# Nearest-neighbour upsampling by two on one core: eight loads of falling size in place of four equal ones

## The chip, the core and the metric

The kernel runs on one core of a Trainium2 chip. The metric is the device time of one execution in microseconds (us). Four executions of the kernel before took 199.92 to 200.24 us, with a median of 200.06. A profile comes from one execution, and its span is the part of that execution between the first and the last recorded work.

## The reference

```python
batch, channels, h, w = (16, 64, 64, 64)        # x, float32
new_h, new_w = (h * scale_factor, w * scale_factor)   # scale_factor = 2
for i in range(new_h):
    for j in range(new_w):
        result[:, :, i, j] = x[:, :, i // scale_factor, j // scale_factor]
```

Every input element is written four times, into a square of two by two. The input has 65,536 rows of 64 numbers (16.78 MB), the output 67.11 MB. Nothing is calculated; the work is moving and repeating.

## The kernel before, in words

The input is seen as 65,536 rows. They are cut into four blocks (`NB`) of 128 partitions x 128 rows, so that a partition's part of a block is 128 neighbouring rows, 32 KiB in one piece. The output is seen the same way: one input row becomes two output rows, 1 KiB in one piece.

**Loads.** Lines 65 to 68 issue all four loads on SP's queue before anything else. Each block has a tile `xt` of its own, so no load waits for anything. The first of these loads is moved by `begin_before_barrier` (lines 9 to 27) to a place ahead of the barrier with which the program begins; it takes the first SP instruction of the body, whatever that is, as long as it is a load without waits.

**Copies.** Lines 74 to 86 go through the four blocks, and in each through four pieces of `K` = 32 rows per partition. For a piece, a tile `u` of 32 KiB per partition is filled: VectorE (DVE) expands the first `KV` = 18 rows (line 78), ScalarE (ACT) the other 14 (line 81). Both read a row with a stride that repeats it and each number in it twice. There are two `u` buffers (`bufs=2`, line 62).

**Stores.** Line 84 stores a `u` tile, again on SP's queue: 128 pieces of 32 KiB, one per partition. Since a partition owns 128 neighbouring rows of a block, the pieces of one store lie 128 KiB apart in the output. A `u` buffer may be filled again when its store has landed.

**Order.** All 20 transfers (four loads, 16 stores) are issued by SP and form one queue, which 16 DMA engines work on in parallel. Each DMA engine has its share of every transfer: eight partitions, so eight data packets and one small one that reports the end. The stores stand in the queue behind all loads.

Of the kernel before, what the change touches and what calls it, by code (L numbers as in the profile page):

```python
# [1 line left out]

# [4 lines left out]


def begin_before_barrier(nc):

    blocks = nc.main_func.blocks
    main, body = blocks[0], blocks[1]
    sp = mybir.EngineType.SP
    load = next(i for i in body.instructions if i.engine == sp)
    assert isinstance(load, mybir.InstDMACopy), type(load)
    assert not (load.sync_info and load.sync_info.on_wait)
    body.instructions = [i for i in body.instructions if i is not load]
    kept = list(main.instructions)  # L20
    at = next(
        n
        for n, i in enumerate(kept)
        if i.engine == sp and isinstance(i, mybir.InstDrain)
    )
    kept.insert(at, load)
    main.instructions = kept


@with_exitstack  # L30
def kernel(
    ctx: ExitStack,
    tc: tile.TileContext,
    x: bass.AP,
    scale_factor: int,
    out: bass.AP,
):
    nc = tc.nc
    nc.at_finalize(begin_before_barrier)
    P = nc.NUM_PARTITIONS  # L40
    s = int(scale_factor)
    B, C, H, W = x.shape
    R = B * C * H
    fdt = x.dtype

    K, J = 32, 4
    NB = R // (P * J * K)  # L50
    assert NB * P * J * K == R
    xf = x.rearrange("b c h w -> (b c h) w").rearrange(
        "(n p r) w -> n p r w", n=NB, p=P
    )
    of = out.rearrange("b c (h hd) w -> (b c h) (hd w)", hd=s).rearrange(
        "(n p r) w -> n p r w", n=NB, p=P
    )

    KV = 18

    xpool = ctx.enter_context(tc.tile_pool(name="xin", bufs=NB))
    upool = ctx.enter_context(tc.tile_pool(name="uexp", bufs=2))

    xts = []
    for n in range(NB):
        xt = xpool.tile([P, J * K, W], fdt, name="xt")
        nc.sync.dma_start(out=xt[:, :, :], in_=xf[n])
        xts.append(xt)

    def expanded(rows):  # L70
        k = rows.shape[1]
        return rows.unsqueeze(2).unsqueeze(4).to_broadcast([P, k, s, W, s])

    for n in range(NB):
        for j in range(J):
            r0 = j * K
            u = upool.tile([P, K, s, W, s], fdt, name="u")
            nc.vector.tensor_copy(  # L78
                out=u[:, :KV], in_=expanded(xts[n][:, r0 : r0 + KV, :])
            )  # L80
            nc.scalar.copy(  # L81
                out=u[:, KV:], in_=expanded(xts[n][:, r0 + KV : r0 + K, :])
            )
            nc.sync.dma_start(
                out=of[n, :, r0 : r0 + K, :], in_=u[:, :, :, :, :]
            )


# [1 line left out]
_INS = ['x', 'scale_factor']  # L90
_OUTS = [((16, 64, 128, 128), 'float32')]

_NUMBERS = {'scale_factor': 2}


# [26 lines left out]
```

## Time and profile before

| what | number |
|---|---|
| median of four executions | 200.06 us |
| the profiled execution | 200.24 us, of which the span is 198.5 us |
| DVE busy, 16 copies of 128x4608 | 40.9 us, 2560 ns each |
| ACT busy, 16 copies of 128x3584 | 50.8 us, 3179 ns each |
| loads | 4 of 4096 KB |
| stores | 16 of 4096 KB, 16.1 us from issue to landing (median) |
| DMA packets | 2880, of which 320 under 512 B and none between 512 B and 8 KB |
| HBM read, written | 16.78 MB, 67.11 MB |
| mean rate over the span | 423 GB/s |

How to read the views: an engine's busy share says how much of the span it worked. A row of 40 digits cuts the span (or a chosen stretch) into 40 equal slices, and each digit is a busy share in tenths. The GB/s row says what the DMA engines moved in each slice. The chain of work that ended last is followed back from the end: each piece has its start, its length and what it was. "SPq" and "ACTq" are the queues of instructions of SP and ACT. "Landing" is the moment at which all the data of a transfer has arrived. In slices shorter than a packet the GB/s row shows bursts and zeros, since a packet's bytes are booked whole.

### The profile page before, as it was taken

The numbers are of one execution on the slowest core, as the hardware profiler recorded it, in microseconds if no ns is written. First come the engines' busy times: TensorE is split into PE (matmuls) and PEld (weight loads), VectorE is DVE, ScalarE is ACT, GpSimd is POOL, SyncE is SP. The second block draws the span as 40 slices with busy tenths as digits, with TensorE's granted clock in tenths as the row PEclk, the third lists the DMA queues.
The fourth block names the chain that finished last, engine by engine and source line by source line (L and its number), as shares of the span: only waits on it lengthen the run. The fifth ranks groups of instructions, "written<-read, shape, count | busy, mean of one in ns | idle before, by whom it ended". The sixth has DMA issues, their size and how long they took to land.

```text
span 198.5 us, 145 instructions
## 1 busy us (share of the span) xinstructions
DVE 40.9 (21%) x16; ACT 52.0 (26%) x17; POOL 0.2 (0%) x4
## 2 busy tenths in 40 slices
DVE  0054000000405050505050505050505050404000
ACT  2057000000415150606060606060606060505000
POOL 0000000000000000000000000000000000000000
DMA  8999999999999999999999999999999999999994
GB/s 317 423 423 423 456 449 456 376 376 423 423 436 443 436 443 429 443 429 429 423 423 436 443 436 443 429 443 429 429 423 423 436 443 436 443 429 443 429 429 211
DMA packets 2880, 83.89 MB, mean 423 GB/s; under 512 B 320, under 2 KB 320, under 8 KB 320
## 3 DMA queue, kind: packets, MB, share of 16 engines
q1 hardware_dynamic: 2880, 83.89, 98.8%
HBM read 16.78 MB, written 67.11 MB: 423 GB/s over the span
## 4 chain that ended last, share of the span: by engine, by line
DMA 77%; ACT 14%; issue 0%; ACTq 0%
DMA out_dram<-u 70%; ACT u L81 14%; DMA xt<-in_x_dram 6%; ACTq L81 0%
## 5 line engine op out<-in xcount | busy, mean ns | idle before, releaser
L81 ACT COPY u<-xt 128x3584 f32<-128x3584 f32 x16 | 50.8, 3179 | 128.5 <-DMA out_dram<-u 118.3
L78 DVE COPY u<-xt 128x4608 f32<-128x4608 f32 x16 | 40.9, 2560 | 139.9 <-DMA out_dram<-u 127.6
L81 ACT ACT_TABLE_LOAD x1 | 1.3, 1283 | 0.8 <-PEq L103 0.8
L103 POOL MEMSET const-uint8-127<- 128x1 uint8 x1 | 0.1, 102 | 0.0
L103 POOL MEMSET const-bfloat16-1.0<- 128x1 bf16 x1 | 0.1, 101 | 0.0
L103 POOL MEMSET const-float32-1.0<- 128x1 f32 x1 | 0.1, 99 | 0.0
L103 POOL MEMSET const-float32-0.0<- 128x1 f32 x1 | 0.1, 98 | 0.2 <-issue 0.2
## 6 DMA issues: line engine op xcount, KB each, us to landing
out_dram<-u SPq DMA_DIRECT2D x16, 4096.0 KB, 16.1
xt<-in_x_dram SPq DMA_DIRECT2D x4, 4096.0 KB, 25.9
```

Source lines behind the costliest of these rows:

```text
L78: nc.vector.tensor_copy(out=u[:, :KV], in_=expanded(xts[n][:, r0 : r0 + KV, :]))
L81: nc.scalar.copy(out=u[:, KV:], in_=expanded(xts[n][:, r0 + KV : r0 + K, :]))
L103: nc = _bacc.Bacc("TRN2", target_bir_lowering=False, num_devices=1)
```

## The change

The rows are cut into eight blocks of 128, 128, 64, 64, 32, 32, 32 and 32 rows per partition. A block has one load, so the pieces that a load moves are 32 KiB per partition in the first two loads, 16 KiB in the next two and 8 KiB in the last four; the loads are of 4096, 4096, 2048, 2048 and four times 1024 KB. All eight are issued at the beginning, and each has a tile with a name of its own in the pool `xin` (`bufs=1`); together these take the same space as the four tiles before. The pieces of 32 rows that are expanded and stored stay 16 in number and equal in size; `KV` and the two `u` buffers stay. What a partition owns changes with the blocks: the stores of a block of 64 rows write 32 KiB pieces that lie 64 KiB apart, and the store of a block of 32 rows writes 4096 KB in one stretch. The function that moves the first load is unchanged, and the first load is the same as before.

```diff
+    blocks = [128, 128, 64, 64, 32, 32, 32, 32]
 
-    K, J = 32, 4
-    NB = R // (P * J * K)
-    assert NB * P * J * K == R
-    xf = x.rearrange("b c h w -> (b c h) w").rearrange(
-        "(n p r) w -> n p r w", n=NB, p=P
-    )
-    of = out.rearrange("b c (h hd) w -> (b c h) (hd w)", hd=s).rearrange(
-        "(n p r) w -> n p r w", n=NB, p=P
-    )
+    K = 32
+    assert P * sum(blocks) == R
 
     KV = 18
 
-    xpool = ctx.enter_context(tc.tile_pool(name="xin", bufs=NB))
+    xf = x.rearrange("b c h w -> (b c h) w")
+    of = out.rearrange("b c (h hd) w -> (b c h) (hd w)", hd=s)
+
+    def of_block(rows, first, k):
+        return rows[first : first + P * k, :].rearrange("(p k) w -> p k w", p=P)
+
+    xpool = ctx.enter_context(tc.tile_pool(name="xin", bufs=1))
     upool = ctx.enter_context(tc.tile_pool(name="uexp", bufs=2))
 
-    xts = []
-    for n in range(NB):
-        xt = xpool.tile([P, J * K, W], fdt, name="xt")
-        nc.sync.dma_start(out=xt[:, :, :], in_=xf[n])
-        xts.append(xt)
+    loaded = []
+    first = 0
+    for n, k in enumerate(blocks):
+        xt = xpool.tile([P, k, W], fdt, name=f"x{n}")
+        nc.sync.dma_start(out=xt[:, :, :], in_=of_block(xf, first, k))
+        loaded.append((xt, first, k))
+        first += P * k
 
...
-    for n in range(NB):
-        for j in range(J):
-            r0 = j * K
+    for xt, first, k in loaded:
+        for r0 in range(0, k, K):
             u = upool.tile([P, K, s, W, s], fdt, name="u")
...
             nc.sync.dma_start(
-                out=of[n, :, r0 : r0 + K, :], in_=u[:, :, :, :, :]
+                out=of_block(of, first, k)[:, r0 : r0 + K, :],
+                in_=u[:, :, :, :, :],
             )
```

More of the change, by code (lines that the diff above doesn't have):

```diff
@@ L70, in expanded @@
-    def expanded(rows):
-        k = rows.shape[1]
-        return rows.unsqueeze(2).unsqueeze(4).to_broadcast([P, k, s, W, s])
-    for n in range(NB):
-        for j in range(J):
-            r0 = j * K
+    blocks = [128, 128, 64, 64, 32, 32, 32, 32]
+    K = 32
+    assert P * sum(blocks) == R
+    KV = 18
+    xf = x.rearrange("b c h w -> (b c h) w")
+    of = out.rearrange("b c (h hd) w -> (b c h) (hd w)", hd=s)
+    def of_block(rows, first, k):
+        return rows[first : first + P * k, :].rearrange("(p k) w -> p k w", p=P)
@@ new lines @@
+    xpool = ctx.enter_context(tc.tile_pool(name="xin", bufs=1))
+    upool = ctx.enter_context(tc.tile_pool(name="uexp", bufs=2))
+    loaded = []
[5 more added lines that the diff above has]
+        first += P * k
+    def expanded(rows):
+        return rows.unsqueeze(2).unsqueeze(4).to_broadcast(
+            [P, rows.shape[1], s, W, s]
+        )
@@ L77 @@
+    for xt, first, k in loaded:
+        for r0 in range(0, k, K):
             u = upool.tile([P, K, s, W, s], fdt, name="u")
             nc.vector.tensor_copy(
-                out=u[:, :KV], in_=expanded(xts[n][:, r0 : r0 + KV, :])
+                out=u[:, :KV], in_=expanded(xt[:, r0 : r0 + KV, :])
             )
             nc.scalar.copy(
-                out=u[:, KV:], in_=expanded(xts[n][:, r0 + KV : r0 + K, :])
+                out=u[:, KV:], in_=expanded(xt[:, r0 + KV : r0 + K, :])
```

## The prediction

> **What bounds the kernel now.** I read the page's engine shares and slices first, then the chain of work that ended last, then the landings of single transfers, and at last the DMA slices around the one place where the rate dips.
>
> ```profile
> DVE 40.9 (21%) x16; ACT 52.0 (26%) x17; POOL 0.2 (0%) x4
> DMA  8999999999999999999999999999999999999994
> GB/s 317 423 423 423 456 449 456 376 376 423 423 436 443 436 443 429 443 429 429 423 423 436 443 436 443 429 443 429 429 423 423 436 443 436 443 429 443 429 429 211
> q1 hardware_dynamic: 2880, 83.89, 98.8%
> ```
>
> The copies take a quarter of the span at most; the DMA engines are at nine tenths or more in every slice but the first and the last, and their packets fill 98.8% of the span. So the time is that of 83.89 MB going through one queue. Whatever does not change how fast that queue drains, when it starts or when it ends, is hidden. A slice is 198.5 / 40 = 4.96 us; the eighth and ninth, 34.7 to 44.7 us, show 376 GB/s where the others show 423 to 456. The chain gives the pace on both sides of that dip:
>
> ```profile
> 0.00 12.26 DMA xt<-in_x_dram
> 12.26 0.02 issue
> 12.28 6.27 ACT u L81 x2
> 18.55 0.02 issue
> 18.57 43.31 DMA out_dram<-u
> 61.88 0.02 issue
> 61.90 0.04 ACTq L81
> 61.94 0.04 issue
> 61.98 3.19 ACT u L81
> 65.17 0.02 issue
> 65.18 16.07 DMA out_dram<-u
> 81.25 0.02 issue
> ```
>
> From 61.88 to 81.25 two stores land: 19.37 us, 9.68 us each, and every later pair of the chain takes 19.36 or 19.37. That is 4.19 MB / 9.68 us = 433 GB/s. The ACT pieces in this chain cost nothing: while one u buffer is refilled, the store of the other is draining. A store takes 16.1 us from issue to landing but they land every 9.68 us, so there is always one queued.
>
> Asked one by one, the loads are issued at 0.0, 0.8, 1.2 and 1.6 us and land 12.3, 21.2, 30.5 and 40.9 us later, so at 12.3, 22.0, 31.7 and 42.5. The second and third take 9.7 us each, the pace of a store. The fourth takes 10.8. The first store (issued at 15.48, 36.7 us to landing) is in at 52.2, and the second at 61.88: 9.7 us each again. So the one loss inside the run is **the turn from loads to stores, 10.8 - 9.7 = 1.1 us, and it falls on the end of the last load**, though two stores have been queued since 18.6 us. DMA slices of 0.18 us show where. First a stretch within loads, from 25.9 to 33.1 us, then the turn, from 35.6 to 42.8 us:
>
> ```profile
> GB/s 1092 1456 364 0 0 0 546 1092 1092 182 0 0 0 728 1092 910 182 0 0 0 1092 1092 546 182 0 0 182 1092 1457 182 0 0 0 546 1092 1092 182 0 0 0
> DMA packets 112, 3.15 MB, mean 437 GB/s; under 512 B 16, under 2 KB 16, under 8 KB 16
> ```
>
> ```profile
> GB/s 1092 1456 182 0 0 0 546 1092 1092 182 0 0 0 910 910 910 182 0 0 0 0 546 910 364 728 364 0 0 0 0 0 182 728 546 728 546 182 0 364 910
> DMA packets 102, 2.82 MB, mean 391 GB/s; under 512 B 16, under 2 KB 16, under 8 KB 16
> ```
>
> The 16 DMA engines take their 32 KiB packets almost in step, so each wave of digits is one packet per engine. Within loads a wave comes every 6 to 7 slices (1.2 us). At the turn, two gaps are long: about 8 slices (from slice 13 to 21) and about 10 (21 to 31). After that the waves are 6 to 7 apart again. Load 4's first wave is the one at 30.6 us (slice 26 above); at 1.2 us each its seventh and eighth are those at slices 13 and 21 of the second row. So two packets per engine, the last two of load 4, run long, and the first store's packets are not the slow ones.
>
> **The change part by part.**
>
> *Issues.* Four more loads on SP: 4 x 0.4 us (the four loads' issues lie between 0.33 and 0.49 us), so SP is busy until about 3.9 us in place of 2.13. Its next work is the first store at 15.48 us; 11 us of cover. If the cover were gone, the store would be issued 1.6 us later, into a queue that is full of loads until 42.5 us: still nothing. The first load is unchanged in size and place, so the first copies start at 12.28 as now.
>
> *Waits of the copies.* The tiles of load 2 are copied from 71.66 us on, those of later loads after 110 us; all loads have landed by about 42.5. Hidden by 50 us and more; no wait is added to the copies or stores that could end last.
>
> *Addresses.* Eight of the 16 stores change from 32 KiB pieces 128 KiB apart to pieces 64 KiB apart (four stores) or adjacent (four). No such store is in the trace. The nearest row is the loads, whose pieces are adjacent: 9.7 us, against 9.68 for spread stores; with landings rounded to 0.1 us the two agree within about 0.07 us, so the bounds are 8 x 0.07 = 0.5 us either way. I take 0: the pace does not show the pattern.
>
> *More packets.* Each transfer is now 8 data packets and a small one per DMA engine (2880 / 16 = 180 = 20 x 9). With 24 transfers that is 216, so 36 packets more per engine, 32 of data and 4 small. The trace has no 8 KiB or 16 KiB load. Lower end 0, if only bytes count. Upper end: the fastest slice of the page is 456 GB/s; if bytes could always go so fast, 4.19 MB would take 9.20 us, and the remaining 0.48 us of a 9.68 us period would be fixed cost of 9 packets, 54 ns each, 36 x 54 ns = 1.9 us. The upper end is generous, since a slice counts whole packets and neighbours of 456 are lower. Loads and stores, with other sources and targets, have the same period, which speaks for bytes; I take 6 ns a packet, near the lower end: **+0.2 us**.
>
> Here a rule of the Trainium skill speaks against the change. "DMA: Bandwidth & Descriptors", section Bandwidth, asks for transfers of 1 MiB or more for 75% of peak, and lists 6.15 us for one of 1 MB; were each of the last four paid at that, they would take 24.6 us instead of 9.7, +14.9 us. The trace weighs against it: the first load lands 2.6 us later than a 9.7 us period explains, and the loads queued behind it do not pay this again. The same page (section on the iDMA fabric) has loads in 4 KiB rows at 408.7 GB/s beside a ceiling of 435.2; my estimate from that is 9.8 ns a packet, and 0.35 us in place of 0.2; no run here shows it.
>
> *The turn.* What remains is the 1.1 us. The two packets that run long are the last two of an engine's load, while the next thing in its queue is a store packet. I read this as packets of both kinds in progress together: once the engine reaches ahead to the store, the load packets still open share it, and what is read early for the store is not won back, since stores go on at the same 9.68 us. If the length of this overlap goes with the size of the load packets still open, packets of 8 KiB leave a quarter of it: 1.1 x 0.25 = 0.27 us, a gain of **0.83 us**. The bounds are 0 (the overlap is set by time or bytes, not by packets) and 1.1 (it vanishes). That the slowdown covers two packets per engine, and not part of one, is what I lean on; it is an inference, as no other packet size stands at a turn. When the stall goes, next is the store pace of 9.68 us, which stays.
>
> *Sum.* +0.2 - 0.83 = -0.6 us. The profiled execution took 200.24 us (span 198.5, 1.7 outside it, which I leave); that gives 199.6 by it. It is the slowest of the four runs; against their median of 200.06 it is 199.45.
>
> **Rivals.**
>
> *The turn does not care (no change).* The overlap is a fixed amount read ahead, or a fixed latency at the change of direction. For it: the long gaps vary from engine to engine, as a latency would. Against it: a pure latency would hardly stretch two packets. Then only the packets' cost is left: 200.06 + 0.2 = 200.26. A gain of 0.5 with costs of 0.3 ends here too.
>
> *Small packets cost more than bytes (slower).* Place: the loads from the third on, half of the 16.78 MB, which must pass before the first store can drain. Price: midway to the upper bound, 27 ns for each of 36 packets, +1.0 us, with an unchanged turn 201.0. It decides (above 200.46) from 11 ns a packet if the turn stays, from 34 ns if the turn gains 0.83. For it: nothing in the trace has packets between 512 B and 32 KiB. Against it: equal periods of loads and stores.
>
> *The loads are not cut as said.* If the smaller rows were handled in the pieces of now, the page would show 2880 packets and the time 200.1. Rows of one partition are what a packet holds today, so I give this nearly nothing and count it with no change.
>
> **How the numbers follow.** A measurement of this kernel can tell 0.2%, 0.4 us, from no change. The turn shrinks: 0.45, between 199.0 (1.1 gained, almost no cost) and 199.65. No change: 0.35, from 199.66 to 200.46. Slower: 0.20, 200.46 to 202.0 (1.9 us of packet cost). Predicted is the likeliest, 199.45; its own range is 199.0 to 199.65. The range of 8 in 10 goes from 199.0 over both first cases into the nearer part of the slower one, 200.6.
>
> **What would show it.** Packets 3456, 384 of them under 512 B. The last load lands near 41.9 us instead of 42.5, and the second store near 61.3 instead of 61.88; all later pairs of stores stay at 19.36 us. If the last load lands at 42.5 or later and the gaps at the turn add up to 1.1 us, the turn step is wrong. If the loads before it land late (the first 8.4 MB at 22.0, the next 4.2 MB at 31.7), the packet cost is wrong. If the pairs of stores change, the address step is wrong.

## The result and the profile after

The changed kernel takes 199.63 us (median of 41 executions, 199.44 to 199.91), the kernel before 199.98 us on the same occasions (61 executions). The ratio is 0.9982, with a 95% interval of 0.9978 to 0.9987: 0.35 us less. That is a real gain, just under the 0.2% that the prediction had called the limit of what can be told; forecast were 199.45 and -0.6 us. The profiled execution took 199.62 us, with a span of 197.8.

From the page of the changed kernel (slices of 4.95 us; packets; the queue's share):

```profile
GB/s 318 424 424 431 421 431 421 416 426 424 424 424 444 451 444 431 437 444 424 424 424 424 424 437 431 457 444 437 437 431 424 424 424 424 424 444 444 451 431 245
DMA packets 3456, 83.89 MB, mean 424 GB/s; under 512 B 384, under 2 KB 384, under 8 KB 384
q1 hardware_dynamic: 3456, 83.89, 99.0%
```

The packets are the 3456 that were forecast. Where the kernel before had two slices at 376, the lowest slice inside the run is now 416, though smaller packets also spread a loss more evenly over the slices. The chain of the changed kernel (start, length, what):

```profile
0.79 21.10 DMA x<-in_x_dram
21.89 0.02 issue
21.91 0.03 SPq L86
21.93 0.03 issue
21.96 39.55 DMA out_dram<-u
61.51 0.02 issue
...
64.82 16.06 DMA out_dram<-u
80.88 0.02 issue
...
119.59 0.02 issue
...
138.95 0.02 issue
...
158.32 0.02 issue
...
177.69 0.02 issue
```

The second store lands at 61.51 us instead of 61.88, and the next pair at 80.88: 19.37 us, as before. The last eight stores are those with new addresses. Up to 119.59 us eight stores have landed; the pairs after it take 19.36, 19.37 and 19.37 us, and the last one, which lands at 197.03, 19.34 (19.35 before). So the difference up to the last landing arose before the stores set their pace, and the stores' new addresses changed nothing. The last two loads, by their issues and their times to landing:

```profile
L68 SPq DMA_DIRECT2D x<-in_x_dram x2: 443/457/471, 3.2 to 3.7; - x2
DMA to landing us min/median/max: 35.9/37.2/38.4
```

They land at 3.2 + 35.9 = 39.1 and 3.7 + 38.4 = 42.1 us. The 1 MB loads ahead of the last land 2.5 us apart, the last one takes 3.0. The turn is shorter, not gone.

But the spans differ by more than this. The span became 0.62 us shorter (198.46 and 197.84 in the trace), the landings from the second store to the last only 0.37 earlier. The other 0.25 us lie behind the last landing, where SP waits for all transfers. SP's instructions of the program's end in the last stretch, first of the kernel before, then of the changed one (count, shortest/median/longest ns, first and last start):

```profile
L117 SPq EVENT_SEMAPHORE  x7: 17/28/28, 197.4 to 198.4; - x7
L117 SPq DRAIN  x3: 7/7/7, 197.7 to 198.0; - x3
```

```profile
L120 SPq EVENT_SEMAPHORE  x7: 17/28/28, 181.4 to 197.8; - x7
L120 SPq DRAIN  x3: 7/7/7, 197.1 to 197.4; - x3
```

Both have seven waits; the first five are for transfers, the last two, among the drains, are not. Before, the first of them is passed only at 197.4 us, when the last store has landed, so the other four for transfers come after it, one every 0.06 us. In the changed kernel the first is passed at 181.4 us, and only the fifth comes after the last landing.

The trace names the counter in which each transfer reports its end. There are eight, used in turn, and the waits at the end ask for them in the same order in both kernels: the fourth first, the eighth last. With 20 transfers the last store reports in the fourth counter; all the later waits are still to be gone through. With 24 it reports in the eighth, and four waits (4 x 0.062 us) are already behind. **The number of transfers, not their size, gave 0.25 us.**

### The profile page after: what moved, and what is told of

It reads as the page before. It is cut to its first block, busy times and chain, and to the rows that moved or that the text cites. A ratio compares the mean times of both kernels' runs of the same rounds, so it can differ in the third digit from the quotient of the medians.

```text
span 197.8 us, 147 instructions
## 1 busy us (share of the span) xinstructions
DVE 40.9 (21%) x16; ACT 52.0 (26%) x17; POOL 0.2 (0%) x4
## 2 busy tenths in 40 slices
DMA packets 3456, 83.89 MB, mean 424 GB/s; under 512 B 384, under 2 KB 384, under 8 KB 384
## 3 DMA queue, kind: packets, MB, share of 16 engines
q1 hardware_dynamic: 3456, 83.89, 99.0%
## 4 chain that ended last, share of the span: by engine, by line
DMA 79%; ACT 11%; issue 0%; ACTq 0%; SPq 0%
DMA out_dram<-u 69%; ACT u L83 11%; DMA x<-in_x_dram 11%; ACTq L83 0%; SPq L86 0%
## 5 line engine op out<-in xcount | busy, mean ns | idle before, releaser
L83 ACT COPY u<-x 128x3584 f32<-128x3584 f32 x16 | 50.8, 3179 | 128.1 <-DMA out_dram<-u 118.0
L80 DVE COPY u<-x 128x4608 f32<-128x4608 f32 x16 | 40.9, 2560 | 139.5 <-DMA out_dram<-u 127.3
```

The lines of the kernel that those rows point to most:

```text
L80: nc.vector.tensor_copy(out=u[:, :KV], in_=expanded(xt[:, r0 : r0 + KV, :]))
L83: nc.scalar.copy(out=u[:, KV:], in_=expanded(xt[:, r0 + KV : r0 + K, :]))
```

## The experiments

The theories: **A**, what is lost at the turn goes with the size of the load packets still open when store packets begin (the prediction's step). **B**, the turn costs a fixed amount and the gain comes from somewhere else. **D** was added after the first four runs: the number of transfers counts. All ratios are to the kernel before, run on the same chip, with 95% intervals.

**The turn without a queued store.** The copies start with the fourth block.

```diff
-    for n in range(NB):
+    for n in [3, 0, 1, 2]:
         for j in range(J):
```

> The kernel before, but the copies begin with the fourth block, so that no store can be queued until the last load has landed; loads unchanged. If the last load packets run long because store packets are already in progress beside them (theory A, and a theory of a fixed amount read ahead as well), the fourth load takes 9.7 us like the others and lands at about 41.4 us instead of 42.5. If they run long for a reason of the loads' own end, it lands at 42.5. The time itself rises by about 4.5 us, since the first store is issued only after 41.4 + 3.2 us.

Measured 204.45 us in one execution. The chain:

```profile
1.66 39.61 DMA xt<-in_x_dram
41.27 0.02 issue
41.29 6.27 ACT u L81 x2
```

The fourth load lands at 1.66 + 39.61 = 41.27 us, not 42.5; in the trace the loads' closing packets end 9.68 us apart, all four. So the last load packets run long only when store packets stand behind them. The turn's loss is overlap with stores, for A as for a fixed amount read ahead.

**The same loads in the opposite order.**

```diff
-    blocks = [128, 128, 64, 64, 32, 32, 32, 32]
+    blocks = [32, 32, 32, 32, 64, 64, 128, 128]
```

> The same eight loads in the opposite order: 8 KiB pieces first, 32 KiB last. Packets stay 3456. Theory A (what is lost at the turn goes with the size of the last load packets): the last packets are 32 KiB again, so the 1.1 us of the turn is back, and the cost of the small packets stays: 0.1 to 0.3 us above the kernel before, ratio 1.0005 to 1.0015. Theory B (the turn costs a fixed amount, and the gain comes from the number of transfers, their addresses or the evenness of the engines): as the changed kernel, ratio about 0.998.

Measured 0.9997 (0.9988 to 1.0006). B's 0.998 is out, and A's range begins at 1.0005, inside the interval but away from its middle. The missing quarter of a microsecond is the end of the program: this kernel has 24 transfers too. Without that, +0.19 us, the price of the small packets.

**Only the fourth load in four, blocks and stores as before.**

```diff
-        nc.sync.dma_start(out=xt[:, :, :], in_=xf[n])
+        cuts = [32, 32, 32, 32] if n == NB - 1 else [J * K]
+        at = 0
+        for k in cuts:
+            nc.sync.dma_start(
+                out=xt[:, at : at + k, :], in_=xf[n][:, at : at + k, :]
+            )
+            at += k
```

> The kernel before, with blocks and stores as they were; only its fourth load is issued as four, each with 32 rows of every partition, so 8 KiB pieces. Theory A: the turn is that of the changed kernel, and without the 16 KiB loads 0.04 us less is paid for packets, so 0.35 to 0.45 us below the kernel before, ratio 0.9978 to 0.9983. If the gain came from the new addresses of the stores, ratio 1.0007, since only the cost of small packets is left.

Measured 0.9984 (0.9975 to 0.9993). As A has it, and the addresses are out; but with 23 transfers 0.18 us of the 0.32 come from the end, as the table below works out.

**Two 16 KiB loads at the end.** `blocks = [128, 128, 128, 64, 64]`.

> Three loads of 32 KiB pieces and two of 16 KiB at the end; no 8 KiB pieces. Theory A with the loss in proportion to the size: half of what 32 KiB to 8 KiB saves or somewhat more (2/3, since 16 KiB is two thirds of the way), so 0.25 us below the kernel before, ratio 0.9985 to 0.999. Theory B: nothing special about 8 KiB, so as the changed kernel or as before.

Measured 0.9999 (0.999 to 1.0008): no gain. The expectation of A missed.

**One load with 8 KiB packets**, twice. A gap of a row after each 32 in the tile cuts the packets while the load stays one transfer.

```diff
...
+        if n == NB - 1:
+            xt = xpool.tile([P, J, K + 1, W], fdt, name="xpad")
+            nc.sync.dma_start(
+                out=xt[:, :, :K, :],
+                in_=xf[n].rearrange("p (j k) w -> p j k w", j=J),
+            )
...
```

> The kernel before with four loads and the same stores; the fourth load stays one transfer, but its tile has a gap of one row after each 32 rows of a partition, so that its packets are 8 KiB. Theory A (size of the last load packets): the gain of the four 8 KiB loads, ratio 0.998 to 0.9985, fourth load landing near 42.1 us. Theory D (what counts is the number of transfers at the turn, each with its small packet): no gain, ratio 1.000 to 1.001, landing at 42.5 us or later.

> The same as the one load with 8 KiB packets, for a second interval and a second profile of its turn. It was 0.9994 (0.9985 to 1.0002). Theory A: a gain, 0.998 to 0.9992, and the turn 0.2 us or more shorter on average than before. Theory D: 1.000 to 1.001.

Measured 0.9994 (0.9985 to 1.0002) and 0.9995 (0.9986 to 1.0005); the load lands at 1.7 + 40.6 = 42.3 and 1.6 + 40.6 = 42.2 us, each to about a tenth. Between A and D both times, and this is where the end was suspected: size alone gives less than four loads of the same size.

**Many transfers, but big packets up to the turn.** The cut of above with `cuts = [120, 2, 2, 2, 2]`: 30 KiB packets, then four transfers of 512 B packets.

> The kernel before, with the fourth load issued as five: 120 rows of each partition (30 KiB packets), then four times 2 rows (512 B packets). As many transfers at the turn as in the changed kernel, but the last 2 us of loads are still one or two big packets per engine. Theory A (the size of the load packets that are open while stores begin): no gain, and 36 packets more at 4 ns or somewhat above, ratio 1.000 to 1.001. Theory D (the number of transfers, or the size of the very last packets): the gain is there, ratio 0.9975 to 0.9985.

Measured 0.9996 (0.9986 to 1.0005), with 0.25 us of it from the end. D is out as an effect at the turn: without the end it is +0.17 us, the packets' price.

**Smaller still.** `cuts = [64, 16, 16, 16, 16]` (4 KiB), `cuts = [96, 8, 8, 8, 8]` (2 KiB), and one transfer with 4 KiB packets (a gap after each 16 rows).

> The kernel before, with the fourth load issued as five: 64 rows of each partition, then four times 16 rows, so 4 KiB pieces in the last 2 MB. Theory A: the loss at the turn falls again, 0.2 to 0.4 us below what 8 KiB leaves, against 36 to 45 packets more than in the kernel before at 4 ns, 0.15 us: ratio 0.9965 to 0.998. A theory of a fixed amount read ahead: no better than 8 KiB, ratio 0.998 to 0.9995.

> The kernel before, with the fourth load issued as five: 96 rows of each partition, then four times 8 rows, so 2 KiB packets in the last 1 MB, about the last 2.4 us of loads. Packets cost 4.3 ns each as measured for 4 KiB, 0.16 us in all. Theory A in proportion: the gain of the 8 KiB and 4 KiB loads or 0.1 to 0.2 us more, ratio 0.997 to 0.998. If about 0.7 us of the turn is fixed, as the profiles with 8 KiB and 4 KiB suggest: ratio 0.9975 to 0.9985, not below.

> The fourth load is one transfer with 4 KiB packets (its tile has a gap of one row after each 16 rows; the copies of this block take 16 rows on each engine, off the path). 56 packets more per engine at 4.3 ns cost 0.24 us. Theory A: a gain of 0.4 us at the turn or more, less 0.24: ratio 0.998 to 0.9995. Theory D: ratio 1.001 to 1.002, since the packets cost and one transfer gains nothing.

Measured 0.9978 (0.9969 to 0.9987), 0.9994 (0.9983 to 1.0004) and 0.9982 (0.9971 to 0.9992). The first lies within what A expected, but 0.25 us of its 0.44 come from the end; the second misses both of its expectations. One transfer with 4 KiB packets gains 0.36 us with nothing from the end, as A expected: the plainest case for size, though SP's first two stores were held up in their issue in this run alone (last section). Its DMA slices at the turn (35.6 to 42.8 us, 0.18 us each), then the same slices of the changed kernel:

```profile
GB/s 410 432 455 364 387 387 432 410 410 410 455 387 387 387 432 410 410 410 455 387 387 387 432 410 341 410 432 159 387 341 842 1115 979 546 0 0 0 910 728 1092
```

```profile
GB/s 410 501 364 501 364 410 364 455 546 364 455 364 410 455 364 546 319 455 364 410 501 273 410 364 46 364 228 319 228 273 410 728 1411 546 546 0 0 0 910 1092
```

The big digits from slice 30 or 31 are the first wave of 32 KiB store packets. With 4 KiB the low stretch before it is slices 24 to 29 with one digit of 159. With 8 KiB it is slices 23 to 29, most of them at 228 to 364 and one at 46. The loss is the sag of loads just before the stores show. Yet 2 KiB packets in the last 1 MB gained nothing at the turn that shows.

**The other side of the turn.** The first store is cut into four of 8 KiB packets, the loads stay.

```diff
-            nc.sync.dma_start(
-                out=of[n, :, r0 : r0 + K, :], in_=u[:, :, :, :, :]
-            )
+            step = 8 if n == 0 and j == 0 else K
+            for q in range(0, K, step):
+                nc.sync.dma_start(
+                    out=of[n, :, r0 + q : r0 + q + step, :],
+                    in_=u[:, q : q + step],
+                )
```

> The kernel before with loads unchanged; only the first store is issued as four, each with 8 of the 32 rows of the tile, so that its packets are 8 KiB. If what is lost is what store packets take while load packets are open, packet by packet, smaller store packets lessen it too: ratio 0.9975 to 0.999 and the fourth load lands before 42.3 us. If only the size of the load packets counts (theory A as recorded), ratio 1.000 to 1.001 and the fourth load lands at 42.5 us.

Measured 0.9993 (0.9984 to 1.0002); the fourth load lands at 1.6 + 40.6 = 42.2 us. With 23 transfers 0.18 us come from the end, so what is left is +0.04, with 27 packets more to pay for: no gain from smaller store packets that shows. The time goes with A as recorded, the landing with the other reading; inconclusive on which side the packets matter.

**Loads and stores side by side.** The second to fourth loads go to ACT's queue.

```diff
-        nc.sync.dma_start(out=xt[:, :, :], in_=xf[n])
+        queue = nc.sync if n == 0 else nc.scalar
+        queue.dma_start(out=xt[:, :, :], in_=xf[n])
```

> The kernel before, but the second to fourth loads are issued by ACT on its own queue, so that stores and loads run side by side from 15.5 us on and not one after the other. If the loss belongs to load and store packets being in progress together, and is paid for as long as they are (1.1 us in about 2.4 us at the turn), the 12.6 MB of loads, mixed with as much of stores over some 55 us, cost 10 us or more: above 205 us. If the loss is paid once, when the queue changes from one to the other and what was read ahead for stores is never used to finish sooner, it is within 0.5 us of the kernel before, either way.

Measured 1.0 (0.9991 to 1.0009).

```profile
0.00 19.52 DMA xt<-in_x_dram
19.52 0.02 issue
19.54 6.27 ACT u L82 x2
25.81 0.02 issue
25.82 35.82 DMA out_dram<-u
61.64 0.02 issue
```

The first load now shares the DMA engines with the others and lands at 19.52 us, and loads and stores run beside one another until the last load, issued at 1.8 us and 56.2 us under way, is in at 58.0. The second store lands at 61.64, 0.24 earlier than in the profile before, and the time is the same. So mixing is not paid for as long as it lasts. The loss is paid once, and the page shows when (slices of 4.95 us):

```profile
GB/s 317 423 423 436 456 364 436 423 423 423 423 423 463 450 436 430 430 436 423 423 423 423 450 443 450 430 436 436 423 423 423 423 423 463 450 436 423 436 436 212
```

The one dip inside the run is the slice from 24.8 to 29.7 us, just after the first store was issued at 22.74. In the trace the load packets of 32 KiB take up to 2.04 us there instead of 1.21, the store packets 1.21 from their first one at 26.68 us. From 30 us on none is stretched, and none at 58 us, where the loads end. So the loss belongs to the beginning of the stores and not to the end of the loads, which fall together in the kernel before.

**All runs in one table.** "End" is the time from the last landing to the end of the span in the trace. "Rest" is the ratio, taken of 200 us, without what the end gives against 1.06 us. "Turn" is from the trace of one execution each: the mean over the 16 DMA engines of how much more than 9.68 us the last 4.19 MB of loads took (the last 8.39 MB and 19.36 us in the changed kernel), less 5 ns for each packet added there (the price is worked out further down).

| kernel | transfers | end us | ratio | rest us | last load packets | turn us |
|---|---|---|---|---|---|---|
| before | 20 | 1.06 | 1 | 0 | 32 KiB | 1.06 |
| changed | 24 | 0.81 | 0.9982 | -0.11 | 8 KiB | 0.66 |
| opposite order | 24 | 0.81 | 0.9997 | +0.19 | 32 KiB | 0.83 |
| 120 rows, four times 2 | 24 | 0.81 | 0.9996 | +0.17 | 30 KiB, 512 B | 1.08 |
| store in four | 23 | 0.88 | 0.9993 | +0.04 | 32 KiB | 0.95 |
| two of 16 KiB | 21 | 1.00 | 0.9999 | +0.04 | 16 KiB | 0.94 |
| fourth load in four | 23 | 0.88 | 0.9984 | -0.14 | 8 KiB | 0.82 |
| one load, 8 KiB | 20 | 1.06 | 0.9994, 0.9995 | -0.12, -0.10 | 8 KiB | 0.81, 0.79 |
| four of 4 KiB | 24 | 0.81 | 0.9978 | -0.19 | 4 KiB | 0.70 |
| one load, 4 KiB | 20 | 1.06 | 0.9982 | -0.36 | 4 KiB | 0.40 |
| four of 2 KiB | 24 | 0.81 | 0.9994 | +0.13 | 2 KiB | 0.87 |
| two queues | 20 | 1.05 | 1.0 | 0 | | |

In these runs the end follows the number of transfers alone: 20, 21, 23 and 24 give 1.06, 1.00, 0.88 and 0.81 us, 0.06 us for each step from the fourth counter to the eighth. The turn is 0.83 to 1.08 us with 30 or 32 KiB, 0.66 to 0.82 with 8 KiB, 0.40 and 0.70 with 4 KiB; so size counts in these profiles, but far less than in proportion. The intervals of the ratios are about 0.2 us wide to each side, and the turns with 32 KiB differ by 0.2 us among themselves, so single rows of "rest" should not be read finely. Both theories have a part in the changed kernel's gain: 0.25 us of 0.35 come from somewhere else than the turn, as B has it, and the rest from the turn.

## Why the prediction came out near, and where its steps failed

**What bounds the kernel: right.** Pairs of stores stay at 19.37 us. Every gain came from before the first store landed or after the last.

**Issues and addresses: right.** SP issues loads until 4.19 us, hidden; the stores kept their pace with each of the two new patterns.

**Waits: one overlooked, without a price.** The prediction saw no added wait that could matter; one was added. SP's own waits in the changed kernel:

```profile
SPq L86 <- DMA x<-in_x_dram: 6.1, 1, 6.1
```

Eight loads take up all eight counters, so the second store uses that of the second load and waits for its landing. It is issued at 21.96 us instead of 18.57, and with the loads lasting until 42.1 us nobody waits for it. It is also why the chain now runs through that load.

**Packets: right.** Forecast 36 x 6 ns = 0.2 us. In the trace an 8 KiB packet takes 309 ns and a quarter of a 32 KiB packet 303; an 8 KiB load of 1 MB takes 2.455 us away from the turn (the first of the four; the next two take 2.48, nearer the turn) against 9.681 / 4 = 2.420, and a 2 MB load of 16 KiB packets 4.862 against 4.841. That is 4 x 0.035 + 2 x 0.021 = 0.18 us, or 5 ns for each of the 36 packets. The run with the opposite order (+0.19) and that with the 512 B packets (+0.17) give the same price in time. The prediction took the Trainium skill's rule of transfers of at least 1 MiB ("DMA: Bandwidth & Descriptors", section Bandwidth) to speak against the change, but the loads of 1024 KB just meet it. The 6.15 us listed there for 1 MB, measured on transfers issued from GpSimd, does not carry over to loads that SP has queued behind others: one takes 2.45 us here. The estimate of 9.8 ns a packet from the same page is too high for this case, where a 0.5 MB load of 4 KiB packets takes 1.249 us against 9.681 / 8 = 1.210: 39 ns for the 7.9 packets more that it has than an eighth of a 32 KiB load, 5 ns each.

**The turn: the direction right, the size wrong.** This is the step that failed: "packets of 8 KiB leave a quarter of it ... a gain of 0.83 us". By the profiles the turn goes from 1.06 to 0.66 us, a gain of 0.40; by the times it is 0.11 + 0.18 = 0.29 us. The two need not agree: the profiled execution of the kernel before, with 200.24 us, lay 0.26 above the median, and its turn is at the long end of the table. The cause, load packets beside queued stores, is shown by the run without a queued store. By the prediction's own signs it came half way: the last load landed at 42.1 us (forecast 41.9, before 42.5), the second store at 61.51 (61.3, 61.88). That the loss shrinks in proportion to the packet is refuted by 16 KiB (0.94 left) and by 4 KiB (0.40 and 0.70). The rival that some of it is a fixed amount paid once holds for the greater part, and the two queues speak for it.

**The end: a term that was missing.** The prediction wrote "span 198.5, 1.7 outside it, which I leave" and costed all behind the last landing at nothing, without asking which waits the added transfers move. It gave 0.25 us, most of the result.

**The sum.** Forecast: +0.2 - 0.83 = -0.6. Measured by term: +0.18 - 0.29 - 0.25 = -0.36, where the turn's -0.29 is itself what the measured ratio leaves. The estimate of the gain was too big and a gain of another origin made up for part of it: the forecast came near partly by luck. The 199.63 us lie 0.02 inside the range up to 199.65, and only because the kernel before, too, measured 0.08 less than the 200.06 that the forecast started from; 0.35 less than 200.06 is 199.71, which the prediction had put down to a turn that does not care.

**Open.** What the fixed part of the turn is (a read-ahead in bytes, or a difference in latency of the two directions) was not separated. Nor why 2 KiB packets did worse than 4 KiB; in its trace the packets sag from 38.3 us on, earlier than the 38.9 of the four loads of 4 KiB packets, and only the last 1 MB had been cut. Nor why four loads of 4 KiB packets left a turn of 0.70 us and one load of the same packets 0.40; each is one profile. In the traces the engines' ends of the last load spread more in the kernel before (0.52 us grows to 0.84) than in the changed one (0.55 stays), and the slowest engine sets the end. Of the 0.37 us by which the second store lands earlier in the profiles, 0.40 - 0.18 = 0.22 are the turn less the packets, taken as a mean over the engines; the other 0.15 go with that evenness, which was not tried on its own, and the 0.29 that the times give hold it too. One load of 4 KiB packets together with 24 transfers, by the table some 0.6 us below the kernel before (0.36 + 0.25), was not tried either; of those run, none is clear of the changed kernel's interval.

## What to carry to other kernels

Where one queue is never empty, read its pace on both sides of every change of direction: the loss is the difference of landings, and only an experiment tells whether it shrinks with the packet size. When a change adds transfers, look at the waits behind the last landing as well: which counter the last transfer reports in can be worth more than the edit itself. And before an effect is put down to what an edit was about, run one kernel that has its side effect alone, here the number of transfers without the small packets.

## What the runs showed of the hardware that was not expected

- **The end of the program.** Each wait that SP has still to pass after the last landing costs 0.06 us; 1.06 us with 20 transfers, 0.81 with 24, the same within 0.01 in all runs with that number.
- **An issue that is held up.** With one load of 4 KiB packets (64 per DMA engine in one transfer) SP's issue of a store took up to 9.58 us instead of 0.33. Count, shortest/median/longest ns:

```profile
L96 SPq DMA_DIRECT2D out_dram<-u x16: 332/332/9577, 15.5 to 181.2; - x16
```

  It was the first store, at 15.5 us; the second, at 25.2, took 4.14, and the loads in the queue hid both. With one load of 8 KiB packets (32 per DMA engine) the first store's issue took 0.36. This points to a limit on the packets that may stand queued, beyond which SP is stopped; the limit itself was not looked for.
- **Stores a little slower with the engines in step.** In the run without a queued store the 16 engines start the stores within 0.17 us of each other instead of 0.4 to 1.1, and the pairs of stores take 19.48 us instead of 19.37 (a store issued at 68.64 lands 16.19 us later, at 84.83; the next of the chain at 104.31). That the one causes the other is not shown.
